# Modulation weights of a hybrid diffusion transformer: more first buffers, another place for three parts, narrower column groups

## The chip, the cores and the metric

The kernel runs on one core of a Trainium2 chip. TensorE (PE) multiplies matrices into PSUM, VectorE (DVE), ScalarE (ACT) and GpSimd (POOL) work element by element, SyncE (SP) issues most transfers, and 16 DMA engines bring data from the chip's main memory (HBM) into SBUF. The metric is the device time of one execution in microseconds; a lower time is better.

## The reference, cut to what matters

Two layers act on 256 latent tokens and 256 context tokens of 1024 features, in float32. Layer 0 has a mixer whose heads are half RWKV-7 and half Mamba-2, fed by one combined input projection to 3312 columns, and then a SwiGLU. Layer 1 has neighbourhood attention and eight SwiGLU experts. Each layer is steered by a modulation: a vector of the latents and one of the context go through SiLU and a matrix of 1024 x 6144.

```python
for i in range(DEPTH):                                   # two layers
    m_lat = split((silu(c)     @ w_ada[i] + b_ada[i]), 6)
    m_ctx = split((silu(c_ctx) @ w_ada[i] + b_ada[i]), 6)
    a_lat = rms_norm(h_lat) * (1 + m_lat[1]) + m_lat[0]   # the context likewise
    o_ctx, o_lat = mixer(a_ctx, a_lat)                    # layer 0: a @ mix_w_in, RWKV-7 | Mamba-2, @ mix_w_out
    h_lat = h_lat + m_lat[2] * o_lat
    h_lat = h_lat + m_lat[5] * channel_mixer(rms_norm(h_lat) * (1 + m_lat[4]) + m_lat[3])
return rms_norm(h_lat)
```

The first third of a layer's modulation (`m[0]` and `m[1]`) is wanted before the layer's first projection, the second (`m[2]`, `m[3]`) behind its mixer, the third (`m[4]`, `m[5]`) at its channel mixer. So of layer 0 only the first third is wanted early.

## The kernel before

**Modulation parts.** The kernel computes the modulation in six parts `(l, q)`: layer `l`, third `q`, 2048 of the 6144 columns each. The weights of a part come in 16 chunks: 128 rows (contraction tile `ko`) by 1024 columns (half `h`), that is 4 KiB for each of 128 partitions, 524 KB in all. `ada_part` (line 301) multiplies: the stationary operand is `cpad`, 32 columns wide (the latents' and the context's vector and zeros), and the weights stream past it. A matmul therefore uses 32 of the array's 128 columns, and the four blocks of 512 output columns lie in four column groups of the array and in four groups of 32 PSUM partitions. A chunk holds two of these blocks, so it has two matmuls over 512 columns (line 309). A float32 matmul is executed as two passes, each a MATMUL record with a weight load of its own: four records a chunk. Behind the 16 chunks a part has a copy from PSUM on VectorE (line 312), four small matmuls that turn it (line 316) and two additions of the bias (line 321).

**Weight stream.** All weights are a list of chunks in order of use. `get_raw` emits their loads up to 15 chunks ahead, all on SyncE's queue; a load waits there, in order, until the buffer that it is to fill has been read for the last time. The first 16 chunks (the part (0, 0)) rotate through five buffers, the later ones of layer 0 through four of 4 KiB per partition, `wraw`. Chunks of a projection are rounded by ScalarE (line 405) and the rest of the rounding is formed by VectorE (line 407), in pieces of half a chunk with four buffers each; the buffer of such a chunk is free when both are done. A modulation chunk is read by TensorE itself, and its buffer is free behind its matmuls.

**Order of the program.** First the tokens are loaded and normed and transposed (lines 254 to 274) and small vectors are turned (276 to 297); then comes part (0, 0) (line 435), the modulated tokens `aS` as a rounding and a rest (lines 439 to 445), and the input projection. Its 14 column groups (`zplan`) have two half groups of 4 contraction tiles each, a chunk for each; `project` (line 411) does 48 matmuls of 128x128 by 256 in a half group (line 428), in turn over PSUM banks "a", "a", "y". Seven groups stand before the Mamba-2 part and seven behind it. The Mamba-2 part takes its PSUM from "b" (three banks) and "ch" (two). Then follow the RWKV-7 mixer of the context, `mixer(0)` (line 1033), the other five modulation parts (lines 1034 and 1035), and the mixer of the latents, `mixer(1)` (line 1042).

**Mixer.** It prepares four head pairs (lines 776 to 851: small matmuls, ScalarE's functions and many VectorE products), inverts blocks on VectorE (lines 871 to 888, 31 steps that need one another), merges the blocks (lines 905 and 911) and scans four chunks of 64 tokens in two halves side by side (lines 915 to 971).

**What sets the order.** The engines run their own instruction streams in order and wait for one another by semaphores. The order within each stream is fixed when the kernel is built: the framework plans it on a simulated timeline (`schedule_with_timeline_sim=True`), where an instruction earlier in the program goes first among those that are ready by that plan. So modulation matmuls that stand behind `mixer(0)` in the program are executed between the mixer's, and where their weights are late on the chip, everything behind them in TensorE's stream waits.

Of the kernel before, what the change touches and what calls it, by code (L numbers as in the profile page):

```python
# [8 lines left out]
F32 = mybir.dt.float32  # L9
F32R = mybir.dt.float32r  # L10
I32 = mybir.dt.int32
AF = mybir.ActivationFunctionType
# [14 lines left out]
def hybrid_kernel(ctx, tc, a, out):  # L27
# [33 lines left out]
    def emit_load(i):  # L61
# [32 lines left out]

    def ada_chunks(l, q):
        return [[chunk(dram(a["w_ada"], (l * D + ko * 128) * 6 * D + q * 2048 + h * 1024, [[6 * D, 128], [1, 1024]]), (1024,))
                 for h in range(2)] for ko in range(KO)]
# [42 lines left out]
    for e in range(NE):  # L140
# [5 lines left out]
        # of the last expert, the features in halves: the first one goes back to the tokens beside the second one's products  # L146
# [24 lines left out]
    wpool = [wsp]  # L171

# [4 lines left out]
    def bank(tag="a"):  # L177
        """a PSUM bank; of several tags in turn"""
# [67 lines left out]
    # columns: silu of the latents' and the context's vector, then zeros  # L246
# [4 lines left out]

# [1 line left out]
    xn = [s0.tile([128, KO, 256], F32, name=f"xn{seg}") for seg in range(2)]  # L253
    for seg in range(2):
        xt = xts[seg]
        ss = s0.tile([128, 2], F32, name="ss", tag="ss", bufs=2)
        for t in range(2):
            S.activation(xn[seg].rearrange("p k t -> p (k t)")[:, 1024 * t:1024 * t + 1024], xt[:, t, :], AF.Square,
                         accum_out=ss[:, t:t + 1])
        V.tensor_scalar(ss, ss, 1.0 / D, EPS, op0=OP.mult, op1=OP.add)  # L260
        S.activation(ss, ss, AF.Sqrt)
        V.reciprocal(ss, ss)
        for t in range(2):
            V.tensor_scalar(xt[:, t, :], xt[:, t, :], ss[:, t:t + 1], None, op0=OP.mult)
        for k in range(0, KO, 2):
            p = bank("b")
            for j in range(2):
                for t in range(2):
                    T.transpose(p[:, 256 * j + 128 * t:256 * j + 128 * t + 128], xt[:, t, 128 * (k + j):128 * (k + j) + 128], ident)
            dst = xn[seg][:, k:k + 2, :].rearrange("p k t -> p (k t)")  # L270
            if k % 4:
                V.tensor_copy(dst, p)
            else:
                S.activation(dst, p, AF.Copy)
# [6 lines left out]
    # sel8[n, h, p] = 1 where n = 2 * h + p // 64  # L281
# [17 lines left out]
    mods = [cst.tile([128, 48, 2], F32, name=f"mod{l}") for l in range(2)]  # L299

    def ada_part(l, q):
        p = bank()
        # blocks of 512 columns beside each other on the array, 32 of its columns each
        for ko in range(KO):
            for h in range(2):
                w = get_raw(ada[l, q][ko][h])
                for x in range(2):
                    j = 2 * h + x
                    T.matmul(p[32 * j:32 * j + 32, :], cpad[:, ko, :], w[:, 512 * x:512 * x + 512], start=ko == 0,  # L309
                             stop=ko == KO - 1, skip_group_check=True)  # L310
        m = c0.tile([128, 512], F32, name="adam", tag="scr", bufs=1)
        V.tensor_copy(m, p)
        p2 = bank()
# [3 lines left out]
        dst = mods[l][:, 16 * q:16 * q + 16, :].rearrange("p (j b) r -> p j b r", b=4)  # L317
        src = p2[:, 0:32].rearrange("p (b j r) -> p j b r", j=4, r=2)
        bias = pv(f"ba{l}", 16 * q, 16).rearrange("p (j b) -> p j b", b=4)
        for r in range(2):  # L320
            V.tensor_tensor(dst[:, :, :, r], src[:, :, :, r], bias, OP.add)
# [7 lines left out]
    # modulation index of a segment: 0 latents, 1 context  # L329
    MOD = (1, 0)  # L330

# [1319 lines left out]
```

## Time and profile before

| | |
|---|---|
| three runs | 2086.82, 2092.52, 2096.49 us; median 2092.52 |
| the profiled execution | span of 2079.9 us from first to last instruction; the profile has no other time of it |
| TensorE (PE) busy | 2000.0 us, 96% |
| its weight loads (PEld) | 1704.1 us, 82% |
| VectorE (DVE) | 1597.2 us, 77% |
| ScalarE (ACT) | 1204.9 us, 58% |
| GpSimd (POOL) | 199.3 us, 10% |
| TensorE's mean granted clock | 0.971 of 2.4 GHz |
| read from HBM | 455.88 MB, 220 GB/s over the span |

Busy time counts the time in which an engine has at least one instruction under way. Matmuls are pipelined and their ends are modelled, so the distance from one start to the next says more about their cost than their own length. The numbers in brackets behind a row are idle time of its engine just before it and what ended that. The chain of waits is followed back from the last instruction of a stretch, at each step to what released it. The granted clock is either 0.50 (1.2 GHz) or 1.00 (2.4 GHz) at a moment; a stretch shows the mean.

### The profile page before, as it was taken

The page shows a single profiled execution, that of the slowest core. Times are in us where ns is not written, and L with a number is a line of the kernel's source. Part 1 is how long each engine was busy: PE and PEld are TensorE (multiplying, and loading weights), DVE is VectorE, ACT ScalarE, POOL GpSimd, SP SyncE. Part 2 cuts the span into 40 slices and gives each one's busy share as a digit, 9 for nine tenths or more (in the row PEclk, how much of TensorE's full clock was granted, in tenths as well). Part 3 has the DMA queues.
Part 4 walks back from the last instruction along what each step waited for, and adds up shares of the span by engine and source line. Part 5 has one row for each costly group of instructions (what it writes and reads, how often), then busy time and mean ns, then how long its engine had stood idle before and what let it go on. Part 6 is the DMA issues. An engine that isn't in the chain of part 4 may idle for free.

```text
span 2079.9 us, 35252 instructions
## 1 busy us (share of the span) xinstructions
PE 2000.0 (96%) x13658; PEld 1704.1 (82%) x13658; DVE 1597.2 (77%) x2559; ACT 1204.9 (58%) x1793; POOL 199.3 (10%) x217
## 2 busy tenths in 40 slices
PE   6999998999999999999999998999999999999997
PEld 3999743668889998999999677888888888888885
DVE  4867667468849855766678666989999999989897
ACT  4444331134434435655568555878787777777775
POOL 3033220013210000000010231000000000000000
PEclk8999999789999998999999998999999999999998
DMA  7333377522333536555555164999999999999991
GB/s 257 98 103 92 125 252 271 183 87 87 92 101 106 168 111 171 180 184 184 173 173 173 61 233 165 375 335 364 327 369 360 349 348 368 354 342 348 350 347 65
DMA packets 266703, 459.33 MB, mean 221 GB/s; under 512 B 13324, under 2 KB 145584, under 8 KB 266528
## 3 DMA queue, kind: packets, MB, share of 16 engines
q1 hardware_dynamic: 257328, 437.75, 61.6%
q0 software_dynamic: 4784, 14.84, 2.4%
q10 hardware_dynamic: 4416, 4.41, 0.8%
q8 instruction: 109, 1.79, 0.3%
q14 instruction: 66, 0.54, 0.1%
HBM read 455.88 MB, written 1.08 MB: 220 GB/s over the span
## 4 chain that ended last, share of the span: by engine, by line
PE 87%; DVE 6%; DMA 4%; issue 1%; ACT 1%; SPq 0%; ACTq 0%; DVEq 0%
PE a L428 25%; PE b L1529 7%; PE b L1530 7%; PE b L1528 7%; PE ch L1579 4%; PE ch L1578 4%; PE ch L1580 4%; PE a L309 3%; PE y L428 2%; DMA wraw<-in_w_ada_dram 2%; PE b L428 2%; DVE wlo L407 2%; PE y L1295 1%; PE a L1151 1%; PE b L1151 1%
## 5 line engine op out<-in xcount | busy, mean ns | idle before, releaser
L407 DVE TENSOR_TENSOR wlo<-wraw,whi 128x1024 fp32r<-128x1024 f32 (+2 forms) x974 | 931.5, 978 | 210.9 <-ACT whi L405 199.5
L405 ACT ACTIVATE whi<-wraw 128x1024 fp32r<-128x1024 f32 (+2 forms) x996 | 831.4, 844 | 443.0 <-PE a L428 232.1
L1529 PE MATMUL b<-wlo,eH 128*128 128x512 f32 (+1 forms) x768 | 288.8, 376 | 1.9 <-DVE wlo L407 1.5
L1530 PE MATMUL b<-whi,eL 128*128 128x512 f32 (+1 forms) x768 | 285.3, 372 | 0.0
L1528 PE MATMUL b<-whi,eH 128*128 128x512 f32 (+1 forms) x768 | 272.4, 374 | 0.0
L428 PE MATMUL a<-xL,whi 128*128 128x256 f32 x928 | 267.1, 288 | 4.4 <-DVE xL L377 4.4
L428 PE MATMUL a<-xH,whi 128*128 128x256 f32 x928 | 267.0, 288 | 2.1 <-ACT xH L375 1.1
L428 PE MATMUL a<-xH,wlo 128*128 128x256 f32 x928 | 266.6, 288 | 0.7 <-DVE wlo L407 0.7
L428 PEld LDWEIGHTS a<-xL,whi 128*128 128x128 f32 x928 | 180.1, 194 | 8.3 <-DVE xL L377 5.3
L428 PEld LDWEIGHTS a<-xH,whi 128*128 128x128 f32 x928 | 180.3, 194 | 5.4 <-ACT xH L375 1.8
L428 PEld LDWEIGHTS a<-xH,wlo 128*128 128x128 f32 x928 | 179.9, 194 | 4.4 <-issue 2.6
L1529 PEld LDWEIGHTS b<-wlo,eH 128*128 128x128 f32 x768 | 144.7, 188 | 29.3 <-DVE wlo L407 5.0
L1528 PEld LDWEIGHTS b<-whi,eH 128*128 128x128 f32 x768 | 144.2, 188 | 26.7 <-ACT whi L405 1.3
L1530 PEld LDWEIGHTS b<-whi,eL 128*128 128x128 f32 x768 | 144.7, 188 | 24.9
L1579 PE MATMUL ch<-wlo,gH 128*128 128x512 f32 x352 | 140.2, 398 | 0.3 <-DVE wlo L407 0.3
L1580 PE MATMUL ch<-whi,gL 128*128 128x512 f32 x352 | 138.9, 394 | 0.0
L1578 PE MATMUL ch<-whi,gH 128*128 128x512 f32 x352 | 116.0, 395 | 0.0
L309 PE MATMUL a<-wraw,cpad 128*32 128x512 f32 x384 | 89.3, 683 | 22.8 <-DMA wraw<-in_w_ada_dram 21.4
L428 PE MATMUL a<-gH,whi 128*128 128x256 f32 x352 | 99.1, 285 | 0.7 <-ACT whi L405 0.3
L428 PE MATMUL a<-gL,whi 128*128 128x256 f32 x352 | 99.0, 284 | 0.4 <-DVE gL L384 0.4
L428 PE MATMUL a<-gH,wlo 128*128 128x256 f32 x352 | 98.5, 284 | 0.0
L1579 PEld LDWEIGHTS ch<-wlo,gH 128*128 128x128 f32 x352 | 66.1, 188 | 16.2 <-DVE wlo L407 1.0
(598 smaller groups left out, 3547.3 us busy)
## 6 DMA issues: line engine op xcount, KB each, us to landing
wraw<-in_moe_w_dram SPq DMA_DIRECT2D x254, 1024.0 KB, 6.5
wraw<-in_w_ada_dram SPq DMA_DIRECT2D x96, 512.0 KB, 5.2
wraw<-in_ffn_w_dram SPq DMA_DIRECT2D x88, 512.0 KB, 3.7
wraw<-in_na_w_qkv_dram SPq DMA_DIRECT2D x40, 512.0 KB, 3.5
wraw<-in_ffn_w_dram SPq DMA_DIRECT2D x48, 384.0 KB, 3.0
wraw<-in_mix_w_in_dram SPq DMA_DIRECT2D x24, 512.0 KB, 3.6
wraw<-in_mix_w_out_dram SPq DMA_DIRECT2D x16, 512.0 KB, 4.3
wraw<-in_moe_w_dram POOLq DMA_DIRECT2D x7, 1024.0 KB, 10.9
```

What stands on the lines that cost most here:

```text
L309: T.matmul(p[32 * j:32 * j + 32, :], cpad[:, ko, :], w[:, 512 * x:512 * x + 512], start=ko == 0, stop=ko == KO - 1, skip_group_check=True)
L405: S.activation(hi, x, AF.Copy)
L407: (G if on_pool else eng or V).tensor_tensor(lo, x, hi.bitcast(F32), OP.subtract)
L428: T.matmul(bs[bi][0:m1 - m0, o:o + 256], w_[:, k, m0:m1], x[part][:, kx, x[2]], start=bi not in begun, stop=last, skip_group_check=True)
L1151: T.matmul(p[:, os_], x[:, ko, ts_], w[:, k, :], start=ko + t == 0 and x is xH and w is wh, stop=ko == KO - 1 and t == 1 and x is xL, skip ...
L1295: T.matmul(O[HALF[p_], 0:256], v1[:, kt, 64 * h:64 * h + 64], PT[:, kt].rearrange("p q t -> p (q t)"), start=kt == 0, stop=kt == 3)
L1528: T.matmul(ps[k][:, 0:w], eH[:, ko, :], wh[:, i, :], start=ko == 0, stop=False)
L1529: T.matmul(ps[k][:, 0:w], eH[:, ko, :], wl[:, i, :], start=False, stop=False)
L1530: T.matmul(ps[k][:, 0:w], eL[:, ko, :], wh[:, i, :], start=False, stop=ko == KO - 1)
L1578: T.matmul(ps[n], gH[:, kf, :], wh[:, w, c_], start=kf == 0, stop=False)
L1579: T.matmul(ps[n], gH[:, kf, :], wl[:, w, c_], start=False, stop=False)
L1580: T.matmul(ps[n], gL[:, kf, :], wh[:, w, c_], start=False, stop=kf == 21)
```

## The change

1. The 16 chunks of part (0, 0) get a buffer each: twelve in tiles of the projection's results and of the modulated tokens, which are written only later (`FIRST`), four in the pool of the start. The norm and the transposes of the tokens stand behind part (0, 0) in the program, no longer before it.
2. Parts (0, 1), (0, 2) and (1, 0) leave the place behind `mixer(0)`. Their 48 chunks are dealt out behind the projection's 28 half groups, one or two at a time (`z_share`), in the weight stream as in the program: `project` calls `between` behind each half group, which takes as many steps of the generator `ada_z`. Their sums lie in a "b" bank until a part is done. Parts (1, 1) and (1, 2) stay behind `mixer(0)`.
3. A chunk has four matmuls over 256 columns, one in each column group, in place of two over 512. The blocks of output columns lie otherwise in PSUM, and the additions of the bias are cut by half instead of by vector.
4. In `zplan` the group "dt" (16 columns) is third, no longer first.

```diff
-            pool_, tag, bufs = (s0, "wr0", 5) if i % 5 < 5 else (zo2, [][i % 5 - 5], 1)
+            pool_, tag, bufs = FIRST[i] if i < len(FIRST) else (s0, "wr0", 2 * KO - len(FIRST))
...
+    FIRST = ([(zo[x], f"{n}T{x}", 1) for x in range(2) for n in "rkv"]
+             + [(zo2, n, 1) for n in ("sz", "xm", "Bm", "Cm")]
+             + [(za, "al1", 1), (za, "ah1", 1)])
...
-    zplan = [("dt", 3296, 16), ("B", 2784, 256), ("C", 3040, 256), ("x", 2272, 256), ("x", 2528, 256),
+    zplan = [("B", 2784, 256), ("C", 3040, 256), ("dt", 3296, 16), ("x", 2272, 256), ("x", 2528, 256),
...
-    zm_ch = [col_chunks(a["mix_w_in"], 0, Z_COLS, c0, w, KS) for _, c0, w in zplan[:ZM]]
-    zr_ch = [col_chunks(a["mix_w_in"], 0, Z_COLS, c0, w, KS) for _, c0, w in zplan[ZM:]]
-    for l, q in ((0, 1), (0, 2), (1, 0), (1, 1), (1, 2)):
+    ADA_Z, ADA_R = ((0, 1), (0, 2), (1, 0)), ((1, 1), (1, 2))
+    z_ch = []
+    rest_ = [(l, q, ko, h) for l, q in ADA_Z for ko in range(KO) for h in range(2)]
+    NZ, NA = 2 * len(zplan), len(rest_)
+    def z_share(n):
+        return (n + 1) * NA // NZ - n * NA // NZ
+    for _, c0, w in zplan:
+        z_ch.append([])
+        for k0 in (0, KO // 2):
+            n = len(z_ch) * 2 - 2 + (k0 > 0)
+            z_ch[-1].append((k0, chunk(w_cols(a["mix_w_in"], 0, Z_COLS, range(k0, k0 + KO // 2), c0, w), (KO // 2, w))))
+            for _ in range(z_share(n)):
+                l, q, ko, h = rest_.pop(0)
+                ada[l, q][ko][h] = ada_chunk(l, q, ko, h)
+    zm_ch, zr_ch = z_ch[:ZM], z_ch[ZM:]
+    for l, q in ADA_R:
         ada[l, q] = ada_chunks(l, q)
...
-    def ada_part(l, q):
-        p = bank()
+    def ada_steps(l, q, tag="a", tag2="a"):
+        p = bank(tag)
         for ko in range(KO):
             for h in range(2):
                 w = get_raw(ada[l, q][ko][h])
-                for x in range(2):
-                    j = 2 * h + x
-                    T.matmul(p[32 * j:32 * j + 32, :], cpad[:, ko, :], w[:, 512 * x:512 * x + 512], start=ko == 0,
-                             stop=ko == KO - 1, skip_group_check=True)
+                for j in range(4):
+                    T.matmul(p[32 * j:32 * j + 32, 256 * h:256 * h + 256], cpad[:, ko, :], w[:, 256 * j:256 * j + 256],
+                             start=ko + h == 0, stop=ko == KO - 1 and h == 1, skip_group_check=True)
+                if ko + h < KO:
+                    yield
...
-    def project(chs, xs, use, w=256, tag="a"):
+    def project(chs, xs, use, w=256, tag="a", between=None):
...
+            if between:
+                between()
...
+    ada_z = (None for l, q in ADA_Z for _ in ada_steps(l, q, "b", "ch"))
+    zn = [0]
+    def between():
+        for _ in range(z_share(zn[0])):
+            next(ada_z)
+        zn[0] += 1
     for i in range(ZM):
-        project(zm_ch[i], aS, z_use(*zplan[i]), w=zplan[i][2], tag="a a y")
+        project(zm_ch[i], aS, z_use(*zplan[i]), w=zplan[i][2], tag="a a y", between=between)
...
     mixer(0)
-    for l, q in ((0, 1), (0, 2), (1, 0), (1, 1), (1, 2)):
+    for l, q in ADA_R:
         ada_part(l, q)
```

## Rows read from the trace of the kernel before

**Rows 1.** The page's first line.

```profile
span 2079.9 us, 35252 instructions
```

**Rows 2.** Stretches: length, busy us (instructions) by engine, clock, DMA share, GB/s.

```profile
...
0.00:20.00 20.00, 8.28 (x31) 3.18 (x33) 5.22 (x19) 7.94 (x15) 11.90 (x26) 0.85 0.92 345
20.00:42.50 22.50, 17.63 (x87) 5.94 (x83) 7.51 (x25) 4.70 (x13) 1.01 (x4) 0.88 0.78 240
42.50:245.90 203.40, 202.76 (x1636) 194.78 (x1639) 155.02 (x333) 92.53 (x170) 54.44 (x68) 0.99 0.31 93
245.90:299.20 53.30, 46.43 (x292) 22.38 (x292) 33.88 (x73) 16.87 (x35) 12.66 (x13) 0.97 0.78 250
299.20:337.90 38.70, 37.45 (x255) 20.32 (x254) 26.08 (x55) 12.03 (x26) 9.40 (x9) 1.00 0.76 253
337.90:370.10 32.20, 22.91 (x112) 6.76 (x110) 27.15 (x70) 3.69 (x6) 0.00 (x0) 0.95 0.87 302
370.10:446.00 75.90, 72.26 (x973) 56.08 (x972) 30.54 (x57) 15.46 (x26) 5.54 (x7) 0.84 0.47 160
...
```

**Rows 3.** TensorE in order of time, the start: from us, length, instructions.

```profile
...
34.51 4.14 PE L309 MATMUL a<-wraw,cpad 128*32 128x512 f32 x12 [1.15 <-DMA wraw<-in_w_ada_dram]
...
42.52 0.40 PE L428 MATMUL a<-ah,whi 128*16 128x256 f32 x1 [2.01 <-ACT ah L443]
...
```

**Rows 4.** SyncE's issues in order of time: the first part's loads.

```profile
...
0.75 28.60 SPq L77 DMA_DIRECT2D wraw<-in_w_ada_dram  x16
...
```

**Rows 5.** The chain of waits from 245.9 to 446, shares by line.

```profile
...
by line: PE a L309 24.9%; DMA wraw<-in_w_ada_dram 23.4%; PE ch L838 2.9%; PE a L316 2.8%; PE b L838 2.7%; PE b L931 2.3%; PE ch L940 2.3%; PE ch L931 2.3%; PE b L849 2.1%; PE ch L867 2.0%; PE b L867 2.0%; PE ch L935 2.0%; PE b L905 1.8%; PE
...
```

**Rows 6.** TensorE's groups, 245.9 to 446: busy, mean ns, idle before.

```profile
...
L309 PE MATMUL a<-wraw,cpad 128*32 128x512 f32 x320 | 71.4, 665 | 18.5 <-DMA wraw<-in_w_ada_dram 18.5
...
```

**Rows 7.** TensorE in order of time: four chunks together, one alone, what follows.

```profile
...
245.85 1.93 PE L309 MATMUL a<-wraw,cpad 128*32 128x512 f32 x16
247.71 0.61 PE L724 MATMUL y<-blk,sqk 128*128 128x2 f32 x4
...
250.96 1.05 PE L309 MATMUL a<-wraw,cpad 128*32 128x512 f32 x4 [1.30 <-DMA wraw<-in_w_ada_dram]
251.94 0.60 PE L347 MATMUL b<-ident,rstd 128*1 128x128 f32 x4
...
```

**Rows 8.** The groups of the same stretch as in Rows 6: line 316.

```profile
...
L316 PE MATMUL a<-ident,adam 128*128 128x8 f32 x40 | 5.7, 270 | 0.9 <-DVE adam L312 0.8
...
```

**Rows 9.** VectorE in order of time, in the inversion.

```profile
...
343.95 0.69 DVE L312 COPY adam<-a 128x512 f32<-128x512 f32 x1 [2.88 <-PE a L309]
...
```

**Rows 10.** A piece of the chain of waits in the projection.

```profile
...
226.37 5.23 PE y L428 x42
...
```

**Rows 11.** The page's DMA issues: count, KB each, median us to landing.

```profile
...
wraw<-in_w_ada_dram SPq DMA_DIRECT2D x96, 512.0 KB, 5.2
...
wraw<-in_mix_w_in_dram SPq DMA_DIRECT2D x24, 512.0 KB, 3.6
...
```

**Rows 12.** The page's groups over the whole span: the rounding on ScalarE.

```profile
...
L405 ACT ACTIVATE whi<-wraw 128x1024 fp32r<-128x1024 f32 (+2 forms) x996 | 831.4, 844 | 443.0 <-PE a L428 232.1
...
```

**Rows 13.** Line 309 alone by stretch: length, PE, PEld, clock, DMA share, GB/s.

```profile
...
299.20:337.90 38.70, 16.61 (x76) 2.34 (x76) 1.00 0.76 253
...
370.10:446.00 75.90, 13.17 (x66) 2.13 (x64) 0.84 0.47 160
...
```

**Rows 14.** TensorE in order of time, in the scan.

```profile
...
404.12 1.05 PE L309 MATMUL a<-wraw,cpad 128*32 128x512 f32 x4 [2.07 <-DMA wraw<-in_w_ada_dram]
...
```

**Rows 15.** Stretches as in Rows 2, cut where the granted clock changes.

```profile
...
375.70:399.60 23.90, 23.90 (x250) 17.76 (x253) 4.67 (x9) 2.94 (x5) 0.00 (x0) 0.50 0.34 111
399.60:447.40 47.80, 44.12 (x590) 33.52 (x578) 21.77 (x47) 10.99 (x20) 5.54 (x7) 1.00 0.50 169
...
```

**Rows 16.** Two pieces of the chain of waits at the scan's start.

```profile
...
370.20 2.04 PE ch L905 x61
...
380.36 3.55 PE b L905 x64
...
```

More of the change, by code (lines that the diff above doesn't have):

```diff
@@ L93, in w_cols, with ada_chunk @@
                     [[rowlen, 128], [128 * rowlen, len(kos)], [1, w]])
+    def ada_chunk(l, q, ko, h):
+        return chunk(dram(a["w_ada"], (l * D + ko * 128) * 6 * D + q * 2048 + h * 1024, [[6 * D, 128], [1, 1024]]), (1024,))
     def ada_chunks(l, q):
-        return [[chunk(dram(a["w_ada"], (l * D + ko * 128) * 6 * D + q * 2048 + h * 1024, [[6 * D, 128], [1, 1024]]), (1024,))
-                 for h in range(2)] for ko in range(KO)]
+        return [[ada_chunk(l, q, ko, h) for h in range(2)] for ko in range(KO)]
     def col_chunks(x, off, rowlen, c0, w, kos):
@@ L111, in hybrid_kernel @@
     ZM = 7
-    zm_ch = [col_chunks(a["mix_w_in"], 0, Z_COLS, c0, w, KS) for _, c0, w in zplan[:ZM]]
-    zr_ch = [col_chunks(a["mix_w_in"], 0, Z_COLS, c0, w, KS) for _, c0, w in zplan[ZM:]]
-    for l, q in ((0, 1), (0, 2), (1, 0), (1, 1), (1, 2)):
+    ADA_Z, ADA_R = ((0, 1), (0, 2), (1, 0)), ((1, 1), (1, 2))
+    z_ch = []
+    rest_ = [(l, q, ko, h) for l, q in ADA_Z for ko in range(KO) for h in range(2)]
+    NZ, NA = 2 * len(zplan), len(rest_)
+    ada.update({lq: [[None, None] for _ in range(KO)] for lq in ADA_Z})
+    def z_share(n):
[10 more added lines that the diff above has]
+    for l, q in ADA_R:
         ada[l, q] = ada_chunks(l, q)
@@ L250, in hybrid_kernel @@
     S.activation(cpad[:, :, 1], p[:, 8:16], AF.Silu)
[L253 to L274, printed above, removed]
     for gi, (t, n) in enumerate(groups):
@@ L316, in ada_part @@
             T.matmul(p2[:, 8 * b:8 * b + 8], m[:, 128 * b:128 * b + 128], pick, start=True, stop=True)
[L317 to L321, printed above, removed]
+        for h in range(2):
+            dst = mods[l][:, 16 * q + 8 * h:16 * q + 8 * h + 8, :].rearrange("p (j b) r -> p j b r", b=2)
+            src = p2[:, 16 * h:16 * h + 16].rearrange("p (b j r) -> p j b r", j=4, r=2)
+            bias = pv(f"ba{l}", 16 * q + 8 * h, 8).rearrange("p (j b) -> p j b", b=2)
+            V.tensor_tensor(dst, src, bias[:, :, :, None].to_broadcast([128, 4, 2, 2]), OP.add)
+        yield
+    def ada_part(l, q):
+        for _ in ada_steps(l, q):
+            pass
+    ada_part(0, 0)
     def scale_cols(l, which, name):
@@ L430, in project @@
                                 begun.add(bi)
+            if between:
+                between()
         for i in range(len(ms)):
             use(i, bs[i] if len(xs) == 2 else bs[0][:, 256 * i:256 * i + 256])
-    ada_part(0, 0)
+    xn = [s0.tile([128, KO, 256], F32, name=f"xn{seg}") for seg in range(2)]
+    for seg in range(2):
+        xt = xts[seg]
+        ss = s0.tile([128, 2], F32, name="ss", tag="ss", bufs=2)
+        for t in range(2):
+            S.activation(xn[seg].rearrange("p k t -> p (k t)")[:, 1024 * t:1024 * t + 1024], xt[:, t, :], AF.Square,
+                         accum_out=ss[:, t:t + 1])
+        V.tensor_scalar(ss, ss, 1.0 / D, EPS, op0=OP.mult, op1=OP.add)
+        S.activation(ss, ss, AF.Sqrt)
+        V.reciprocal(ss, ss)
+        for t in range(2):
+            V.tensor_scalar(xt[:, t, :], xt[:, t, :], ss[:, t:t + 1], None, op0=OP.mult)
+        for k in range(0, KO, 2):
+            p = bank("b")
+            for j in range(2):
+                for t in range(2):
+                    T.transpose(p[:, 256 * j + 128 * t:256 * j + 128 * t + 128], xt[:, t, 128 * (k + j):128 * (k + j) + 128], ident)
+            dst = xn[seg][:, k:k + 2, :].rearrange("p k t -> p (k t)")
+            if k % 4:
+                V.tensor_copy(dst, p)
+            else:
+                S.activation(dst, p, AF.Copy)
     g0m = scale_cols(0, 1, "nm0")
@@ L733, in hybrid_kernel @@
     for chs, z in zip(zr_ch, zplan[ZM:]):
-        project(chs, aS, z_use(*z), w=z[2], tag="a a y")
+        project(chs, aS, z_use(*z), w=z[2], tag="a a y", between=between)
         if z[:2] == ("v",1280):
```

2 lines of the change are left out of this document (1 added, 1 removed).

## The prediction

> **What bounds the kernel now.** I read the stretches first, then the chain of waits, then TensorE's own order of work in the places that the change touches. All of it lies in the first 446 of 2079.9 us [rows 1]; nothing behind that is edited. The reader should see four different limits there [rows 2].
>
> Up to 42.5 us the kernel waits for the first modulation part: its last weights reach TensorE at 34.51 and the projection begins at 42.52 [rows 3]. The transfers ran at 345 GB/s in the first 20 us and at 240 in the rest [rows 2], because the five buffers let SyncE issue the sixteen loads only by 29.4 us [rows 4]. From 42.5 to 245.9 TensorE is full, 202.8 of 203.4 us, while DMA moves 93 GB/s [rows 2]. Only from 245.9 to 446 is there much to win: five modulation parts (80 chunks) run beside the context's mixer, and the chain of that stretch goes 24.9% through line 309, 23.4% through its weights' transfers and 2.8% through line 316 [rows 5]. Of the 200 us TensorE spends 71.4 in line 309 and sits 18.5 idle before it [rows 6]. Within it the limits differ: VectorE has 27.2 of 32.2 us in the inversion (337.9 to 370.1), and TensorE 72.3 of 75.9 in the scan behind it [rows 2].
>
> **The change part by part.** *Sixteen buffers.* All sixteen loads can be issued at once. They are 16 x 0.524 = 8.4 MB; the tokens beside them are 2.1 MB. At the 345 GB/s of the first 20 us [rows 2], 10.5 MB take 30.4 us, so the last chunk lands near 31.2 and its matmuls end near 32.2. Before, they ended at 34.51 + 4.14 = 38.65 [rows 3]. The 3.9 us from there to the projection (copy, line 316, additions, first modulated tile) stay. Gain 6.4; I take 6. The ends are 9 (TensorE then has the 32 token transposes left to hide) and 0 (the tokens' normalisation, now written behind this part, comes late and takes the cover's place).
>
> *Four column groups a chunk.* A chunk was two matmuls over 512 columns, each of two passes; it becomes four over 256. What four groups side by side do is shown already where chunks of both halves meet: 16 passes from 245.85 to 247.71, 1.86 us for four chunks. A chunk alone takes 250.96 to 251.94, 0.98 us [rows 7]. With b for a bundle of passes that run together and s for what a visit costs, 2b + s = 0.98 and 4b + s = 1.86 give b = 0.44 and s = 0.10. Passes half as long, in two bundles of four groups: 0.44 + 0.10 = 0.54 us a chunk, 0.98 for two in a row. The ends: 0.465 (the four chunks' mean), and 0.98 if the new groups do not run together.
>
> The row gives four groups their full factor of four. The Trainium skill ("TensorE: Matmul & The Clock Gate", "Measured speedup vs the span model") reports 2.38 for three column groups and 3.07 for four row groups. If four column groups did 3.07, as an estimate by that page a chunk would take 8 x 0.22 / 3.07 + 0.10 = 0.67 us, and the next item 6 us more; since the trace has the thing itself, I stay with 0.54.
>
> *Three parts inside the projection.* 48 chunks over 28 half groups: twenty gaps get two, eight get one. TensorE has 0.6 us free in that stage [rows 2], so all of it is on the path: 20 x 0.98 + 8 x 0.54 = 23.9, and three times line 316 (5.7 us for five parts [rows 8], 1.1 each) is 3.4. Together +27; the ends are 24 (no cost of a visit, a little filled into the start, where TensorE waits for modulated tiles) and 31. VectorE's three copies of 0.69 us [rows 9] and six additions lie beside this: VectorE is busy 155 of 203 us there [rows 2]. Without that cover they would cost 3.
>
> Each added load waits on SyncE for one of the four common buffers, and behind it in SyncE's queue stand the projection's own loads; for these wait ScalarE's rounding (line 405), VectorE's rest (line 407) and TensorE. A buffer of a modulation chunk comes free only when TensorE reaches it. In a gap of two, the load of half group n+2 can start when the second chunk behind half group n is done, and TensorE wants it after half group n+1 and two more chunks. A half group is 48 matmuls; 42 took 5.23 us [rows 10], so 48 take 6.0, and the lead is 6.0 + 1.0 = 7.0 us. A lone projection load lands in 3.6, a modulation load in 5.2 [rows 11], and the rounding adds 0.8 [rows 12]: 4.4 to 6.0. So it holds, by 1 to 2.6 us, until ScalarE or VectorE are late by that much. Cost of a miss: from below 0; from above the chain's transfer share in the old modulation stage, 23.4% of 200 us over 80 chunks [rows 5], 0.59 us a chunk, 28 us for 48; TensorE's own idle there, 18.5 us over 80 [rows 6], makes 11. I take 4, nearer to 0, since the lead is longer than the landing. The bank that an open part holds (one of the three that the Mamba part uses) I cost at nothing, because TensorE has the projection to do meanwhile; it is a part of the 28.
>
> *What the later stretch gives back.* 32 chunks are left of 80. The last 80 were loaded at about 250 GB/s, 2.1 us a chunk [rows 2], and four lie ready at the start, so 28 still need 59 us: up to about 305 this stretch is paced as before. Halved matmuls free TensorE, but VectorE and the transfers go on: 53.3 becomes 52. In 299.2 to 337.9 line 309 takes 16.6 us of TensorE [rows 13], VectorE is busy 26.1 [rows 2], and the rest is round trips between the engines that stay: 38.7 becomes 35. In the inversion VectorE stands 2.88 us before the copy of a modulation part [rows 9] and then makes it; 32.2 becomes 28. In the scan TensorE is the limit and every interruption counts: 13.2 us of line 309 [rows 13], 2.1 of idle before it at 404.12 [rows 14], 2.3 of line 316 (two parts): 18. Against this stands the clock. It was 1.2 GHz (granted 0.50) from 375.7 to 399.6 and 2.4 after [rows 15], and line 905 took 2.04 us before the fall and 3.55 behind it [rows 16]. With no modulation matmuls to do, TensorE is idle during the inversion, and I let the fall come earlier, at the cost of the first 5 us of the scan: +4. Net 14. Sum 1 + 4 + 4 + 14 = 23. The ends: 34, if the stages shrink to 46, 34, 28 and 58 (VectorE's busy time and the round trips); 10, if the transfers pace all of the preparation and the clock costs twice that.
>
> **Sum.** -6 + 27 + 4 - 23 = +2 us on the profiled execution, 2082. That span is 12.6 us under the median of the runs, 2092.5, which also hold what lies around it; the same difference kept, 2095. The halved matmuls and the better cover are spent on work that moved from a stretch where half of it was hidden into one where none is.
>
> **The rivals.** *Faster.* The later stretch is held by its modulation work more than I allow: lines 309 and 316 and the transfers are 51% of its chain [rows 5], and TensorE's order there puts mixer steps behind chunks that have not landed. For it speaks the 18.5 us of idle; against it VectorE's 118 us of 200 in the same stretch and its serial inversion. With the upper end, -6 + 24 + 0 - 34 = -16: 2077.
>
> *Slower: four buffers starve the projection.* Place: the first seven column groups, where TensorE has nothing else. It decides from the point at which a projection chunk is landed and rounded more than 7 us after its buffer came free; VectorE is busy 76% of that stage, so a queue of 2 us before the rounding's rest is enough. Price by the end above: 28 in place of 4, so +26: 2119. Against it: 25 MB more over 231 us make some 190 GB/s, under the 250 to 302 that the same four buffers carried later [rows 2].
>
> *Slower: the clock stays low.* With the modulation matmuls gone from the end of the stretch, TensorE could stay at 1.2 GHz from the inversion to the end of the scan. From 399.6 to 447.4 it is busy 44.1 us [rows 15], some 37 without modulation work; most of it would double as line 905 did: about +30, 2125. Against it: behind the rise the scan held 2.4 GHz for 48 us with thin modulation work. The Trainium skill ("TensorE: Matmul & The Clock Gate", "HAM oscillation") says that gaps in TensorE's work bring the half clock back. By that rule the clock would be low when the scan begins, as I assume; the trace does not show it, since line 309 ran in the inversion.
>
> *The change does not do what it says:* the four groups run two by two. Then each chunk costs 0.44 more, 21 us in the projection: 2116. [Rows 7] speak against it.
>
> **How the numbers follow.** About 10 us, 0.5%, is what the runs of this kernel can tell from no change (they lie between 2086.8 and 2096.5). Chances: the forecast 0.41, the faster rival 0.28, the starved projection 0.20, the clock 0.08, the column groups 0.03. So faster by over 0.5% 0.28, within 0.41, slower 0.31. The forecast's own range is 2084 to 2104. The range for 8 in 10 takes in the faster rival with the spread of the runs below it, 2068, and reaches to the starved projection, 2121; the clock's price and the lower half of a deeper gain are left out.
>
> **What would show it.** The projection's first matmul at 36 to 37 us; line 309 as eight passes a chunk, 0.5 to 0.6 us; the projection's stage 27 to 31 us longer, with no idle before its matmuls; line 309 over by some 55 us after the projection's end; the inversion without the 2.88 us wait; granted clock 0.50 at the start of the scan and 1.00 within its first third. TensorE idle on the projection's weights for over 10 us in sum, or a scan at 0.50 to its end, would make me wrong upwards; a stretch of mixer and modulation under 170 us, downwards.

## The result, and the profile after

The changed kernel takes 2150.6 us (median of 4 runs, 2145.5 to 2158.0) against 2094.5 for the kernel before on the same chip: ratio 1.0278, 95% interval 1.0243 to 1.0312, so 58 us slower by the ratio (56 between the medians). I had forecast 2095, with a range up to 2121. The first line of the page after stands against [rows 1]: the profiled executions differ by 66.0 us.

```profile
span 2145.9 us, 36009 instructions
```

Cut at the first projection matmul, at the last one, and at the end of the first mixer pass (its second write of the mixer's output), the two executions and those of two experiments (below) compare so, in us: e2_front_only, which is the kernel before with the first edit alone, and e1_one_bank, the most telling one.

| stage | forecast of the difference | before | e2_front_only | after | e1_one_bank |
|---|---|---|---|---|---|
| start, to the first projection matmul | -6 | 42.5 | 35.8 | 37.3 | 36.7 |
| projection | +31 | 203.1 | 203.1 | 281.7 | 246.4 |
| from there to the first pass's end | -23 | 208.3 | 221.7 | 204.0 | 216.0 |
| the rest | 0 | 1626.0 | 1627.8 | 1622.9 | 1633.3 |
| span | +2 | 2079.9 | 2088.4 | 2145.9 | 2132.4 |

The profile before is one of the shortest executions of its kernel: in the later profiles the run's time is 1.7 to 1.9 us above the span, so it stands for some 2082 us, under all four runs above, and its mean clock of 0.971 is that of the shortest runs (of the 29 runs of the kernel before beside e1_one_bank, the four under 2086 us had 0.971 to 0.973, the seven over 2098 us 0.953 to 0.963). Behind the start e2_front_only is therefore the better yardstick; its time is that of the kernel before (ratio 0.9990). Against it the differences are +1.5, +78.6, -17.7 and -4.9, in sum 57.5, which is the 58 of the runs.

The start did what was forecast. The loss is the projection's 78.6 us. The stretch behind it gave back less than the 23 us forecast: 4 against the profile before, 18 against e2_front_only. The rest, where nothing is edited, lies between 1623 and 1635 us in all the kernels run here. The stretches of the kernel after answer to [rows 2] and, in the last two, to [rows 15] (length, busy us by engine, granted clock, DMA share, GB/s):

```profile
...
37.30:201.20 163.90, 155.12 (x1328) 136.30 (x1328) 102.54 (x216) 60.25 (x113) 29.80 (x40) 0.98 0.57 178
201.20:266.90 65.70, 48.96 (x284) 36.63 (x284) 40.45 (x100) 20.01 (x35) 24.18 (x30) 0.77 0.16 44
266.90:319.10 52.20, 50.27 (x424) 45.52 (x424) 20.58 (x40) 13.72 (x28) 0.02 (x1) 0.92 0.63 206
319.10:375.80 56.70, 48.30 (x376) 28.62 (x370) 28.00 (x67) 15.43 (x32) 11.43 (x12) 0.77 0.73 246
375.80:422.80 47.00, 44.03 (x254) 30.88 (x254) 34.22 (x61) 14.87 (x31) 12.47 (x11) 0.66 0.38 115
422.80:446.00 23.20, 4.18 (x32) 3.26 (x32) 21.11 (x62) 3.72 (x6) 0.00 (x0) 0.69 0.00 0
446.00:523.00 77.00, 71.61 (x907) 62.91 (x908) 36.91 (x60) 14.18 (x25) 3.03 (x5) 0.70 0.06 17
...
431.80:486.40 54.60, 37.39 (x486) 35.69 (x486) 31.03 (x57) 6.46 (x11) 0.00 (x0) 0.50 0.01 1
486.40:508.50 22.10, 22.10 (x375) 20.33 (x375) 10.53 (x23) 3.91 (x7) 0.00 (x0) 1.00 0.01 3
...
```

The second row is the odd one: for 65.7 us in the middle of the projection DMA moves 44 GB/s and TensorE idles for 17. TensorE in order of time shows why (start us, length us, instructions, idle before it), beside the rows that answer to [rows 3] and [rows 7]. L307 is the modulation matmul (L309 before), L436 the projection (L428), L316 the rearranging, L748 the last use of a `b` bank in the Mamba part:

```profile
...
33.39 1.06 PE L316 MATMUL a<-ident,adam 128*128 128x8 f32 x8 [0.56 <-DVE adam L312]
...
37.31 0.58 PE L436 MATMUL a<-ah,whi 128*128 128x256 f32 x1 [1.87 <-ACT ah L475]
...
57.07 1.07 PE L307 MATMUL b<-wraw,cpad 128*32 128x256 f32 x16
58.07 0.50 PE L436 MATMUL a<-ah,whi 128*128 128x256 f32 x2
...
63.91 0.64 PE L307 MATMUL b<-wraw,cpad 128*32 128x256 f32 x8 [2.14 <-DMA wraw<-in_w_ada_dram]
64.48 0.50 PE L436 MATMUL y<-ah,whi 128*128 128x256 f32 x2
...
177.54 0.64 PE L307 MATMUL b<-wraw,cpad 128*32 128x256 f32 x8
...
244.69 1.88 PE L316 MATMUL ch<-ident,adam 128*128 128x8 f32 x8
...
261.35 2.07 PE L748 MATMUL b<-rowst,ones 1*128 1x512 f32 x2 [0.77 <-DVE rowst L356]
263.35 3.64 PE L307 MATMUL b<-wraw,cpad 128*32 128x256 f32 x32
...
```

Part (0,2) has its last chunk at 177.54. The next modulation matmul comes 86 us later, at 263.35, right behind the Mamba part's last `b` bank, and it is four chunks in a row: all four weight buffers had been full of chunks of part (1,0). Line 316 of part (0,2), into a `ch` bank, stands at 244.69 among the Mamba part's last `ch` uses. SyncE's issues show the jam from the other side (the first row answers to [rows 4]):

```profile
...
0.75 19.59 SPq L77 DMA_DIRECT2D wraw<-in_w_ada_dram  x16
...
178.24 7.87 SPq L77 DMA_DIRECT2D wraw<-in_w_ada_dram  x2
264.49 0.38 SPq L77 DMA_DIRECT2D wraw<-in_mix_w_in_dram  x1
...
```

From 186 to 264 no weight is asked for. The projection runs out of rounded weights at 201.2 and takes up again at 269.

### The profile page after: what moved, and what is told of

Its sections match the earlier page's. It is cut to its first block, busy times and chain, and to the rows that moved or that the text cites. A ratio compares the mean times of both kernels' runs of the same rounds, so it can differ in the third digit from the quotient of the medians.

```text
span 2145.9 us, 36009 instructions
## 1 busy us (share of the span) xinstructions
PE 2024.0 (94%) x14042; PEld 1741.6 (81%) x14042; DVE 1601.8 (75%) x2559; ACT 1204.4 (56%) x1793; POOL 198.2 (9%) x217
## 4 chain that ended last, share of the span: by engine, by line
PE 72%; DVE 5%; issue 1%; ACT 1%; DMA 1%; ACTq 0%; DVEq 0%
PE a L436 21%; PE b L1569 7%; PE b L1570 7%; PE b L1568 7%; PE ch L1619 4%; PE ch L1620 4%; PE ch L1618 4%; PE b L436 2%; DVE wlo L415 1%; PE y L1335 1%; PE a L1191 1%; PE b L1191 1%; PE a L1577 1%; PE ch L1325 1%; PE a L1469 1%
## 5 line engine op out<-in xcount | busy, mean ns | idle before, releaser
L415 DVE TENSOR_TENSOR wlo<-wraw,whi 128x1024 fp32r<-128x1024 f32 (+1 forms) x974 | 929.2, 977 | 251.4 <-ACT whi L413 239.9
L413 ACT ACTIVATE whi<-wraw 128x1024 fp32r<-128x1024 f32 (+1 forms) x996 | 829.2, 843 | 484.8 <-PE a L436 214.9
L436 PE MATMUL a<-xH,whi 128*128 128x256 f32 x928 | 267.1, 288 | 4.2 <-DVE su L1132 2.7
L436 PE MATMUL a<-xL,whi 128*128 128x256 f32 x928 | 267.0, 288 | 2.4 <-DVE xL L385 2.2
L436 PE MATMUL a<-xH,wlo 128*128 128x256 f32 x928 | 266.5, 288 | 0.6 <-DVE wlo L415 0.6
L436 PEld LDWEIGHTS a<-xH,whi 128*128 128x128 f32 x928 | 180.3, 194 | 7.7 <-DVE su L1132 2.9
L436 PEld LDWEIGHTS a<-xL,whi 128*128 128x128 f32 x928 | 180.0, 194 | 6.5 <-DVE xL L385 3.4
L436 PEld LDWEIGHTS a<-xH,wlo 128*128 128x128 f32 x928 | 179.9, 194 | 4.2 <-issue 2.6
L436 PE MATMUL a<-gH,whi 128*128 128x256 f32 x352 | 99.1, 285 | 1.1 <-ACT whi L413 0.8
L436 PE MATMUL a<-gL,whi 128*128 128x256 f32 x352 | 99.0, 284 | 0.4 <-DVE gL L392 0.4
L436 PE MATMUL a<-gH,wlo 128*128 128x256 f32 x352 | 98.5, 284 | 0.0
L1620 PEld LDWEIGHTS ch<-whi,gL 128*128 128x128 f32 x352 | 66.0, 188 | 15.0
```

Of the source, the lines that this page charges most:

```text
L413: S.activation(hi, x, AF.Copy)
L415: (G if on_pool else eng or V).tensor_tensor(lo, x, hi.bitcast(F32), OP.subtract)
L436: T.matmul(bs[bi][0:m1 - m0, o:o + 256], w_[:, k, m0:m1], x[part][:, kx, x[2]], start=bi not in begun, stop=last, skip_group_check=True)
L1620: T.matmul(ps[n], gL[:, kf, :], wh[:, w, c_], start=False, stop=kf == 21)
```

## The experiments

Theory A: the spread parts ask for their banks behind the Mamba part's, and this stops them, the four buffers and the projection. B: four buffers for two streams starve the projection whatever the bank. C: the Mamba part is slow on two `b` banks. Each ratio is to the kernel before, run on the same chip in turn.

**e1_one_bank.**

```diff
+    held = bank("b")
+    ada_z = (None for l, q in ADA_Z for _ in ada_steps(l, q, held=held))
...
-        p = bank(tag)
+        p = held if held is not None else bank(tag)
...
-        p2 = bank(tag2)
+        p2 = held if held is not None else bank(tag)
```

> The kernel after, but the three spread parts use one bank of the three, taken before the first column group, kept until the last spread part is done, and used for the part's sums and then for its rearranged columns; nothing is asked for behind the Mamba part's banks any more. Theory A (a bank that is handed out behind the Mamba part's banks stops the chunk of part (1,0), its four weight buffers, and with them the projection): the stop from 201 to 266 us goes, TensorE has projection matmuls beside the Mamba part again, the projection ends near 268 us instead of 320, and the time is 2080 to 2102 us. Theory B (four weight buffers shared by two streams are too few, whatever bank is used): a stop of 30 us or more stays somewhere in the projection, and the time is 2125 us or more. Theory C (the Mamba part is slow on two banks instead of three): its last product (the second use of the last b bank) still comes at 255 us or later with TensorE waiting, 2130 to 2150 us.

Measured: 2133.1 us, ratio 1.0179 (1.0143 to 1.0215). The stop is gone: no gap of over 4 us between projection matmuls. So A holds for the stop, and it costs 0.99% or 21 us, give or take 10. But the time is outside what A gave, and in B's and C's range: 37 us of loss are left. B's stop did not come. The Mamba part's last `b` bank is done only at 286.6, as C has it, but TensorE does not wait for it: it is busy 239.8 of the projection's 246.4 us. Two stretches, then the three steps of the scan between its copies at 432.5, 451.1, 465.0 and 474.4:

```profile
...
36.70:283.10 246.40, 239.81 (x2026) 208.82 (x2030) 158.35 (x349) 92.87 (x174) 55.69 (x69) 0.99 0.56 173
283.10:355.10 72.00, 63.41 (x403) 37.07 (x403) 30.13 (x73) 15.79 (x32) 10.97 (x12) 0.62 0.64 208
...
432.50:451.10 18.60, 18.36 (x232) 17.36 (x232) 3.06 (x8) 2.96 (x6) 0.00 (x0) 0.50 0.00 1
451.10:465.00 13.90, 13.28 (x163) 12.80 (x165) 4.76 (x11) 1.75 (x3) 0.00 (x0) 0.62 0.01 2
465.00:474.40 9.40, 9.40 (x168) 9.00 (x166) 4.73 (x11) 1.18 (x2) 0.00 (x0) 1.00 0.01 3
...
```

Its groups of TensorE over the projection (busy, mean ns), and ScalarE's longest wait in 42 to 245 (us, times, longest):

```profile
...
L307 PE MATMUL b<-wraw,cpad 128*32 128x256 f32 x364 | 31.0, 398 | 0.0
L316 PE MATMUL b<-ident,adam 128*128 128x8 f32 x16 | 1.9, 245 | 0.0
...
```

```profile
...
ACT whi L413 <- DMA wraw<-in_mix_w_in_dram: 54.5, 19, 7.3
...
```

The projection is 43.3 us longer than before. TensorE is busy 37 us more in it: 32.9 are the spread parts' own matmuls, 1.9 are small ones that came over from the start (lines 276 and 291), and the others are spread over many lines. It idles 6 us more. Of its waits there only 1.0 us is for a rounded weight; the longest are for steps of the Mamba part (us, times, longest):

```profile
...
PE b L670 <- ACT Btk L662: 2.7, 1, 2.7
...
PE b L698 <- DVE Sst L690: 1.2, 1, 1.2
PE a L436 <- ACT whi L413: 1.0, 1, 1.0
...
```

So ScalarE's long waits for weights reach TensorE by 6 us at the most.

**y4_own_sums_bank**: the kernel after, with half of that edit.

```diff
-        p2 = bank(tag2)
+        p2 = p if tag == "b" else bank(tag2)
```

> The kernel after with one half of the one-bank edit: a spread part's rearranged columns go into its own sums' bank (of tag b) and no longer into a bank of tag ch; each part still asks for a new bank of tag b. If part (1,0)'s request for a b bank behind the Mamba part's is what stops it, the stop stays (no spread chunk between the end of part (0,2) and the last Mamba use of a b bank, 60 us or so) and the time is 2140 to 2155 us. If the wait for a ch bank is the cause, the stop is gone and the time is as e1_one_bank's, 2125 to 2138 us.

Measured: 2150.9 us, ratio 1.0289 (1.0240 to 1.0338), as the kernel after. The stop stays, and part (1,0) again starts right behind the Mamba part's last `b` bank (TensorE in order of time):

```profile
...
190.10 0.62 PE L307 MATMUL b<-wraw,cpad 128*32 128x256 f32 x2
194.65 0.95 PE L316 MATMUL b<-ident,adam 128*128 128x8 f32 x8
...
255.61 2.07 PE L748 MATMUL b<-rowst,ones 1*128 1x512 f32 x2 [0.77 <-DVE rowst L356]
257.61 3.64 PE L307 MATMUL b<-wraw,cpad 128*32 128x256 f32 x32
...
```

So it is the request for a `b` bank, not the `ch` bank.

**e2_front_only**: the kernel before with `FIRST` (sixteen buffers) and the tokens' norm moved, as in the change's diff.

> The kernel before with the first edit alone: the first sixteen modulation chunks in sixteen buffers, the tokens' norm behind them in the program. If the 5.2 us by which the projection starts earlier in the kernel after are a gain for the whole, the ratio to the kernel before is 0.9970 to 0.9980 (5 us of 2094). If the gain is given back by the first projection loads or by a later clock, it is 0.999 to 1.001.

Measured: 2090.7 us, ratio 0.9990 (0.9960 to 1.0020). The projection starts at 35.8 and ends at 238.9, 6.7 earlier, but the first pass ends at 460.6 (before 453.9). The program behind the start has the same text, so it also shows how far one execution differs from another in that stretch. Its stages (preparation in two halves, inversion, the rest) took 49.3, 43.2, 26.8 and 89.0 us in the profile before, at clocks of 0.97, 1.00, 0.94 and 0.83; here

```profile
...
238.90:296.00 57.10, 53.59 (x269) 26.07 (x269) 30.02 (x70) 16.94 (x34) 11.60 (x13) 0.79 0.71 224
296.00:339.10 43.10, 41.11 (x273) 22.96 (x272) 31.78 (x57) 12.51 (x26) 9.57 (x9) 0.96 0.67 224
339.10:367.10 28.00, 21.19 (x102) 6.63 (x100) 22.08 (x67) 3.84 (x6) 0.00 (x0) 0.89 0.86 302
367.10:460.60 93.50, 87.75 (x1005) 61.68 (x1004) 41.29 (x70) 16.39 (x29) 5.57 (x7) 0.81 0.45 150
...
```

A gain of 5 us and none cannot be told apart.

**e3_four_groups**: the kernel before with the change's `ada_part` (eight matmuls of 256 columns a chunk).

> The kernel before with four column groups a chunk alone: all five late parts stay beside the first mixer pass, each chunk takes eight matmuls of 256 columns, four side by side. If TensorE sets the pace there, its modulation time goes from 71 us to about 50, and of that 8 to 15 us come off the end: 2080 to 2087 us. If the weights' transfers or the mixer's own chain set it, the time stays within 4 us of before; if a TensorE that is less busy falls to the lower clock earlier, it is 5 to 15 us slower than before.

Measured: 2097.2 us, ratio 1.0017 (0.9993 to 1.0041). Over 245.9 to 454, where all but 28 of the 640 records lie, the matmuls keep TensorE 65.4 us, against 71.4 in [rows 6], with the same idle time before them, which the transfers end. The clock was lower in this execution (0.72 in the first half of the preparation), which hides a part of what the narrower matmuls save:

```profile
...
L309 PE MATMUL a<-wraw,cpad 128*32 128x256 f32 x612 | 65.4, 497 | 18.7 <-DMA wraw<-in_w_ada_dram 18.7
...
```

So TensorE's time in these matmuls does not set the pace there: the second expectation, that the weights or the mixer's own chain do.

**e4_no_spread.**

```diff
-    ADA_Z, ADA_R = ((0, 1), (0, 2), (1, 0)), ((1, 1), (1, 2))
+    ADA_Z, ADA_R = (), ((0, 1), (0, 2), (1, 0), (1, 1), (1, 2))
```

> The kernel after with no part spread over the projection: all five late parts behind the first mixer pass, as in the kernel before; sixteen first buffers, four column groups and the order B, C, dt of the first column groups stay. Theory A and B alike: the stop of 62 us is a matter of the spread parts, so it is gone, and the time is the sum of the two other edits: 2075 to 2092 us. If the first edit or the column groups had a part in the loss (another order of the projection's first loads, a lower clock), it stays over 2100 us.

Measured: 2097.6 us, ratio 1.0030 (1.0003 to 1.0057). The expected gain did not come, but the loss is 0.6% at the most: nearly all of the 58 us lies in the spread.

**x1_no_late.** The kernel before without its five late parts.

```diff
-    for l, q in ((0, 1), (0, 2), (1, 0), (1, 1), (1, 2)):
-        ada[l, q] = ada_chunks(l, q)
...
-    for l, q in ((0, 1), (0, 2), (1, 0), (1, 1), (1, 2)):
-        ada_part(l, q)
```

> The kernel before without its five late modulation parts: neither their weights are loaded nor their matmuls done, and the modulations they give are left at zero, so the output is not the reference's. Before, the stretch from the projection's end (245.6) to the end of the first mixer pass (453.9) is 208 us. If the late parts lengthen it by TensorE's time, as the prediction had it (23 us for three of the five), it shrinks to about 170 us and the time is 2050 to 2062 us. If they hide in time in which TensorE would wait for the mixer's own chain, it stays within 10 us of 208 and the time within 10 us of before (2084 to 2104), the more so if TensorE without them shows the lower granted clock over more of the stretch.

Measured: 2064.2 us, ratio 0.9869 (0.9829 to 0.9910), so all five parts cost 27 us (19 to 36 by the interval). The stretch is 184.3 us, in place of 208.3 in the profile before and 221.7 in e2_front_only. Both expectations missed, the time lies between them. The four stages without late parts:

```profile
...
247.00:290.40 43.40, 36.68 (x163) 29.51 (x164) 29.34 (x69) 16.84 (x35) 12.51 (x13) 0.53 0.09 22
290.40:330.80 40.40, 37.09 (x184) 28.77 (x184) 30.64 (x54) 13.38 (x27) 9.90 (x9) 0.66 0.02 4
330.80:353.90 23.10, 4.23 (x32) 3.31 (x32) 21.02 (x61) 3.15 (x5) 0.00 (x0) 0.66 0.00 1
353.90:431.30 77.40, 71.92 (x907) 62.91 (x908) 37.00 (x61) 14.18 (x25) 3.03 (x5) 0.70 0.06 17
...
```

The clock is lower as well: with less to do TensorE is granted 0.53 to 0.70, where the stages with five parts had 0.83 to 1.00 in the profile before and 0.79 to 0.96 in e2_front_only.

**y1_one_bank_no_late**: e1_one_bank without its last two parts (`ADA_R`).

> The one-bank kernel without its last two modulation parts, neither loaded nor computed; the modulations they give are left at zero, so the output is not the reference's. In e1_one_bank the stretch from the projection's end to the first pass's end is 216 us; in x1_no_late, with none of the five, it was 184. If the two parts that are left cost as much as the five did in the kernel before (24 us) because all their chunks come right behind the projection, ahead of the key norms and the first preparations and at the lower clock, the stretch is 180 to 188 us and the time 2098 to 2108. If the stretch is long for another reason (the clock after a TensorE with little to do), it stays over 200 and the time over 2118.

Measured: 2099.6 us, ratio 1.0056 (1.0033 to 1.0079); the stretch is 181.2 us. The two parts that are left cost 26 us by the ratios in e1_one_bank, give or take 9 (35 in the stretches of the profiles): about as much as the five did before, as expected. Most of it lies ahead of the inversion's input, 72.0 us there, and here

```profile
...
282.40:327.50 45.10, 37.98 (x180) 30.26 (x181) 29.77 (x71) 15.84 (x33) 11.73 (x12) 0.58 0.14 42
327.50:363.10 35.60, 31.52 (x184) 24.66 (x183) 30.53 (x54) 13.13 (x27) 9.32 (x9) 0.77 0.03 4
...
```

**y2_one_bank_late_behind**: e1_one_bank with those two parts behind the operands.

```diff
-    for l, q in ADA_R:
-        ada_part(l, q)
+    with tc.issue_after(behind[0].ins):
+        for l, q in ADA_R:
+            ada_part(l, q)
```

Here `behind[0]` is the last transpose of `operands` in the first pass.

> The one-bank kernel with the last two modulation parts queued on TensorE behind the last transposes of the first mixer pass's operands, so that their 32 chunks lie beside the inversion and the scan instead of ahead of the key norms. If their place is what lengthens the stretch, the preparation (from the projection's end to the inversion's start, 115 us in e1_one_bank) shrinks to about 85, the scan grows by 3 to 10 us, and the time is 2105 to 2120 us. If they only change place (merge and scan wait for chunks as long), it stays within 5 us of 2133.

Measured: 2112.5 us, ratio 1.0105 (1.0061 to 1.0149). The preparation takes 84.3 us, the scan 61.0 (53.6 in e1_one_bank); all as the first expectation. Beside the inversion two parts cost less, not nothing: it takes 29.0 in place of 23.1 us.

```profile
...
283.10:327.90 44.80, 37.81 (x181) 30.10 (x181) 29.11 (x70) 15.53 (x32) 11.71 (x12) 0.58 0.11 30
...
367.40:396.40 29.00, 21.01 (x164) 8.47 (x164) 21.64 (x62) 3.15 (x5) 0.00 (x0) 0.64 0.74 267
...
```

**x2_touch**: e1_one_bank with a copy in place of the spread chunks' matmuls.

```diff
+                G.tensor_copy(jk, get_raw(ada[l, q][ko][h])[:, 0:1])
```

> The one-bank kernel (e1_one_bank) with the 48 spread chunks loaded as there, in the same order and the same four buffers, but each read by one copy of a single column on POOL in place of its eight matmuls; the three modulations are left at zero, so the output is not the reference's. In e1_one_bank the projection runs from 36.7 to 283.1 (246 us, before 203). If TensorE's own time for the spread chunks is the cost, the projection ends at 240 to 250 and the time falls by 30 us or more, to 2095 to 2105. If the loads (twice the bytes through four buffers) are, it still ends at 265 or later and the time stays over 2115.

Measured: 2100.9 us, ratio 1.0057 (1.0028 to 1.0086); the projection ends at 269.2, so each theory has one number right. The edit is not clean: no bank is held, so the Mamba part has its third `b` bank again, and POOL's copies wait for the weights, with the Mamba part's own work on POOL behind them (waits in 42 to 245). It says no more than that the loads alone can cost something; it does not size them.

```profile
...
POOL jk L574 <- DMA wraw<-in_w_ada_dram: 121.4, 41, 6.4
...
PEld b L693 <- POOL xdd L691: 12.0, 3, 10.2
...
```

**y3_one_bank_ring5**: e1_one_bank with five buffers.

```diff
+        elif i < 2 * KO + NZ + NA and i % 5 == 4:
+            pool_, tag, bufs = zw, "wz", 1
```

> The one-bank kernel with five weight buffers instead of four while the projection runs (each fifth chunk lies in a buffer of its own). In e1_one_bank ACT waits 54.5 us for the projection's weights between 42 and 245 us. If the ring of four costs the part of the z stage that the chunks' own matmuls (about 32 us of the 43 that it is longer than before) don't, the projection ends 5 to 12 us earlier than 283 and the time is 2120 to 2128 us. If the transfers' rate sets it, nothing changes: within 3 us of 2133.

Measured: 2121.3 us, ratio 1.0152 (1.0112 to 1.0191), not to be told from e1_one_bank's 1.0179. ScalarE's wait for the projection's weights falls from 54.5 to 24.2 us, and the projection ends 3.5 us earlier, less than expected: most of that wait was hidden. TensorE's idle time in the projection falls from 6.6 to 2.9 us.

```profile
...
ACT whi L417 <- DMA wraw<-in_mix_w_in_dram: 24.2, 7, 7.7
...
```

**x3_one_bank_warm** and **x4_before_warm**: e1_one_bank and the kernel before, with idle work at each step of the inversion.

```diff
+                pace = T.matmul(pf[:, 0:32], ident, Xu[:, s + 1, :], start=True, stop=True)
+                with tc.issue_after(pace.ins):
+                    for x in range(2):
+                        T.matmul(pf[:, 256 * x:256 * x + 256], ident, PV[:, 0:256], start=True, stop=True)
```

> The one-bank kernel with idle work for TensorE in the first mixer pass's inversion: at each of its 31 steps one small matmul that reads the step's row and two of 256 columns on constants, into a bank that nobody reads. In e1_one_bank the granted clock is 0.5 from 406.9 to 461.5, over the inversion's end and most of the scan. If the lower clock, after a TensorE without modulation work, ate the gain in the mixer's stretch, the clock is 1.0 when the scan begins, the scan is 10 to 20 us shorter and the time 2112 to 2123 us. If the clock is not what lengthens it, the time stays within 4 us of 2133.

> The kernel before with the same idle work in the inversion. Before, the clock is 0.5 from 447.4 to 467.9 and 375.7 to 399.6; modulation matmuls run beside the inversion. If the clock is what counts, the gain is small here because those matmuls do the same already: 0 to 8 us, 2086 to 2094. If the idle work delays the late parts behind the scan, 5 us or more slower.

Measured: 2140.0 us, ratio 1.0225 (1.0184 to 1.0266), and 2102.9, 1.0068 (1.0036 to 1.0101): 10 and 14 us slower than without. The idle work was too long. In x3 VectorE ends the inversion at 423.35, and the first matmul behind it, at 423.19 in e1_one_bank, comes 15 us late (in x4 the inversion ends at 376.3 and that matmul comes at 391.8):

```profile
...
438.32 2.11 PE L953 MATMUL ch<-X,AA 32*32 32x32 f32 x61
...
```

And in x3 the clock fell all the same, 1.4 us after the scan's start at 442.4:

```profile
...
399.50:443.80 44.30, 44.02 (x368) 39.13 (x366) 32.62 (x70) 6.78 (x11) 0.00 (x0) 1.00 0.00 1
443.80:471.10 27.30, 25.90 (x318) 24.66 (x319) 6.35 (x13) 4.12 (x7) 0.00 (x0) 0.50 0.01 2
...
```

So these two leave open what a scan at full clock from its first step would gain.

## Why the prediction was wrong

**The step that failed.** "The bank that an open part holds (one of the three that the Mamba part uses) I cost at nothing, because TensorE has the projection to do meanwhile; it is a part of the 28." I looked at the bank that is held and not at the bank that is asked for. In the program, part (1,0)'s request stands behind every `b` request of the Mamba part, and it was served behind them. TensorE does not have the projection to do meanwhile, because the projection's weights stand in SyncE's queue behind four chunks that cannot be used. Price: 1.0278 to 1.0179, 21 us, give or take 10; e1_one_bank takes the stop away, y4 shows that the `b` request makes it without the `ch` request. In the profiles the projection is 35 us shorter without the stop, the stretch behind it 12 longer and the rest 10. The 12 lie in the first half of the preparation (72.0 us at a clock of 0.62 in e1_one_bank, 56.7 at 0.77 in the kernel after); why, no run here shows.

**The spread's own cost.** Forecast 27 for its matmuls and 4 for its loads. Without the stop the stage is 43.3 us longer. The matmuls are 32.9 of it (31.0 and 1.9 in e1_one_bank), 6 over the forecast. The loads are near the 4 that I took: TensorE idles 6 us more, and a fifth buffer brings 3.5 back. The rival of the starved buffers had the right queue and the wrong place: not the first seven column groups, but the stop behind them.

**The gain that was mis-sized.** I let three of five parts give back 23 us. In the kernel after the stretch gave back between 4 (against the profile before) and 18 (against e2_front_only). By the runs, leaving out all five gives 27 (x1): most of their 71.4 us on TensorE [rows 6] lay beside other work. And the two that stay cost 26 in e1_one_bank (y1). Where the modulation went away the gain came about as forecast: the inversion from 26.8 us (28.0 in e2_front_only) to 23.2 (forecast 4), the scan, from its first matmul to its last state update, from 64.5 to 53.3 (forecast 14, with the clock). A part of it was given back ahead of them. In the kernel after the two halves of the preparation took 56.7 and 47.0 us: 11 more than in the profile before, 3.5 more than in e2_front_only, where I had forecast 5 less. Of the 34 chunks that are left behind the projection (the last two spread ones among them) 26 run in the first of these halves, between the key norms and the first preparations, many of them at the lower clock, where a chunk takes some 1.0 us and not 0.57. The last one comes 77 us behind the projection's end, not 55:

```profile
...
326.25 1.08 PE L307 MATMUL a<-wraw,cpad 128*32 128x256 f32 x8
...
396.03 0.64 PE L307 MATMUL a<-wraw,cpad 128*32 128x256 f32 x8
...
```

**Two readings.** I took the 12.6 us between the profile before and the runs for what lies around the span; only some 1.8 do, and the others are that execution's own. The forecast of 2095 keeps the whole difference, so this does not move it. And the lower end of the gain, 10, is the scan's alone; with the inversion's 4, which it leaves out without a word, it is 14.

**The clock.** Forecast +4 us for the scan. Steps two and three of the scan in e1_one_bank do the same work, in 13.9 us with 10.4 of them at 0.50, and in 9.4 at 1.00: 0.43 us for each us at the lower clock. From 430.5 to 461.5 that makes 13, an estimate. In the kernel after, the clock is 0.50 from 431.8 to 486.4, over 31 us of the scan. This is the clock rival in part: it rose before the scan's end, and the scan without chunks is still the shorter. In the inversion ahead of that scan TensorE had 4.2 of 23.2 us to do (19.5 of 26.8 in the profile before). The rule of the Trainium skill that I had weighed ("TensorE: Matmul & The Clock Gate", "HAM oscillation"), that gaps bring the half clock back, agrees with this row. But x3 shows the fall without such a gap, so gaps are not all of it.

**What was right.** The start: projection at 37.3, forecast 36 to 37. A chunk in four column groups: 0.57 us alone, 1.00 for two (forecast 0.54 and 0.98), so four groups ran side by side as in [rows 7]. The 0.67 us that the prediction estimated from the 3.07 of the Trainium skill ("TensorE: Matmul & The Clock Gate", "Measured speedup vs the span model") does not fit the 0.57 measured. The inversion without its 2.9 us wait. But neither the start nor the column groups are worth anything that can be measured in the time (e2, e3, e4).

No complete version here beats the kernel before beyond what can be measured; the start alone (0.9990) is the nearest.

## What to carry to other kernels

When work is interleaved into a stage, follow each buffer it will ask for, not only those it holds: a request that stands in the program behind another part's requests for the same pool can be served behind that whole part, and everything queued behind it waits too. Take such a bank once, ahead of both. And before pricing what moved work gives back, ask what leaving it out altogether would give (here 27 us for all of it), and where the part of it that stays will now run.

## What the runs showed of the hardware

In the kernel after and in e1, x1, x2 and y1 the scan runs without modulation beside it. TensorE is busy in it nearly all the time, and yet each of the five ran its first 30 to 31 us at the lower clock and the rest at the full one, some 54 us in all. Work ahead of the scan did not keep the clock up: in x3 TensorE was busy for 44.0 of the 44.3 us ahead of the fall, at the full clock, the merge behind the inversion and the scan's first matmuls among them.
